# Down projection of a decoder block on one Trainium2 core: another order of its seven products, alternating banks, three sets of split activations

## The chip, the cores and the metric

The kernel runs on one core of one Trainium2 chip. A core has a matrix engine (PE; its weight loads are listed as PEld), a vector engine (DVE), a scalar engine (ACT), a general engine (POOL), and a queue that issues transfers (SP). ACT can issue transfers too; a `q` behind an engine's name in the profile is its queue. All transfers of the core run on the same 16 DMA engines. The metric is the device time of one execution in microseconds. "The clock" is the share of PE's full clock that was granted.

## What is computed

One decoder block over 1024 tokens of width 1024, all in float32: two token mixers, their merge, and a gated feed-forward network. The change lies in the last product of the feed-forward network and in what follows it:

```python
h = rms_norm(x, norm_ffn_g[l]) * (1.0 + sc2) + sh2
gt, up = jnp.split(jnp.einsum("bsd,df->bsf", h, w_ffn_up[l]), 2, axis=-1)
x = x + g2 * jnp.einsum("bsf,fd->bsd", jax.nn.silu(gt) * up, w_ffn_down[l])
...
return rms_norm(x, final_norm_g)
```

The activations `silu(gt) * up` are 1024 × 2816, `w_ffn_down` is 2816 × 1024.

## The kernel before

PE multiplies float32 in three passes: each operand is split into a part that PE takes directly (`hi`) and a rest (`lo`), and hi·hi, lo·hi and hi·lo are summed in PSUM. ACT makes `hi` by a copy, DVE makes `lo` by a subtraction. So every operand costs one ACT and one DVE instruction before PE can use it.

**Seven products.** Up and down projection use a Strassen scheme. Activations and weights are each cut into four quadrants (X11 ... X22 by token half and by even or odd 128-wide block of the inner dimension; W11 ... W22 by the same blocks and by column half), and seven products of sums of quadrants replace eight. For the down projection the operands on the activations' side (X11, X12, X22 and the sums XS1 to XS4) are made by DVE during the up projection, in `act_out`, and stored to seven arrays `act_d` in DRAM. The up projection runs over 22 blocks `f` of 128 inner columns; at odd `f` the sums XS1, XS2, XS4 follow from two successive blocks. ACT's queue issues these stores. The operands on the weights' side are formed from quadrants loaded anew for each product: `WSTEP[i]` names, for product i, a quadrant that is loaded into the buffers `reg0` to `reg5` (`w_fetch`, "fresh"), a second one that is loaded into `other`, and the sign with which they are combined (`w_form`); then ACT and DVE split the result into the tiles `wd`.

**Tiles.** Product i has four tiles t, one for each 128 tokens of a token half, so n = 4i + t runs from 0 to 27. The activations of tile 0 are prepared by `x_first`. For the others `x_fetch` loads 704 KB into `xr` (two buffers), `x_split` makes `xh` on ACT and `xl` on DVE (two sets), and `down_mm` runs 11 × 3 matmuls into one PSUM bank: `xh`·`wd` hi, `xl`·`wd` hi, `xh`·`wd` lo (lines 1345 to 1347). `evict` (and `last` in the last product) adds the bank into the partial sums `U` and `V` (one pair for each t) and, where a quarter of the output is complete, multiplies by the row `g2row`, adds the token rows `x1`, takes the sum of squares on ACT, and multiplies by the row `grow`. When both column halves of a token block are done, `store` takes the inverse root on POOL, scales the two halves on DVE and ACT, and issues two stores from SP.

**Order.** The products run as X11, XS1, XS2, X22, XS3, XS4, X12. The loop below issues, for each n: the fetch for n + 2, token rows, the split of n + 1, the forming of a part of the next product's weights, fetches for the product after, and then the matmuls and the eviction of n. A scheduler then sets the order in which instructions stand on each engine, from the data they depend on, their place in this loop, and simulated durations; each engine works strictly in that order, and SP's queue too.

**Banks.** `bank()` hands out eight banks in turn: pc, pa, pn, pc and then both halves of a pair `mm`, both halves of another pair. A pair is one tile to the scheduler, so whoever writes one half waits until the readers of the other have ended.

**SBUF.** The pool `fp` of the down projection takes the place of the pools of the up projection (`ups`, `trs`), so its first tiles wait until the readers of those are done.

Of the kernel before, what the change touches and what calls it, by code (L numbers as in the profile page):

```python
# [12 lines left out]
OP = mybir.AluOpType  # L13
# [30 lines left out]
X11, XS1, XS2, X22, XS3, XS4, X12 = range(7)  # L44
# [3 lines left out]
WSTEP = ((), (W12, W11, 1), (None, W22, -1), (None, W21, 1), (W22, W12, 1), (W22, None, 0), (W21, None, 0))  # L48
# [7 lines left out]
def hybrid_block(ctx: ExitStack, tc: tile.TileContext, x, c, w_ada, b_ada, norm_mix_g, w_in, b_in,  # L56
# [904 lines left out]
    act_d = [dram.tile([128, 4, FP, 128], F32, name=f"act_d{i}") for i in range(7)]  # L961
# [201 lines left out]
    def act_out(f, half, cg, cu):  # L1163
        ts_ = slice(0, 4) if half is None else slice(2 * half, 2 * half + 2)

        def out(i, t):
            nc.scalar.dma_start(act_d[i][:, ts_, f // 2, :], t.rearrange("p (a c) -> p a c", c=128))
# [9 lines left out]
        out(X22, cg[1])  # L1177
        nc.vector.tensor_add(x21, x21, cg[1])
# [4 lines left out]
        out(XS4, s4)  # L1183

# [21 lines left out]
    def x_first():  # L1206
        out = []
        for a, b in ((0, KT), (KT, FP)):
            raw, hi, lo = (wp.tile([128, KT, 128], dt, name=n, tag=n)[:, 0:b - a, :]
                           for n, dt in (("wraw", F32), ("whi", F32R), ("wlo", F32R)))  # L1210
            nc.sync.dma_start(raw, act_d[X11][:, 0, a:b, :])
# [82 lines left out]
    x1 = [fp.tile([128, D], F32, name=f"x1_{t}") for t in range(8)]  # L1294
    ss = fp.tile([128, 8, 4], F32, name="ssf")
    grow, g2row = (fp.tile([128, D], F32, name=n) for n in ("grow", "g2row"))
# [25 lines left out]
    def x_fetch(n):  # L1322
        raw = fp.tile([128, FP, 128], F32, name="xr", tag="xr", bufs=2)
        nc.sync.dma_start(raw, act_d[n // 4][:, n % 4])
        return raw

    def x_split(raw):
        hi, lo = (fp.tile([128, FP, 128], F32R, name=n, tag=n, bufs=2) for n in ("xh", "xl"))
        nc.scalar.activation(hi, raw, AF.Copy)  # L1329
        nc.vector.tensor_sub(lo, raw, hi.bitcast(F32))  # L1330
        return [(hi[:, k, :], lo[:, k, :]) for k in range(FP)]
# [24 lines left out]
    def store(t):  # L1356
        rsqrt(ss[:, t, 3:4], ss[:, t, 2:3])
        r = ss[:, t, 3:4]
        rows = out2[t * 128:(t + 1) * 128, :]
        for i, (a, b) in enumerate(HALVES):  # L1360
            if i:
                nc.scalar.activation(x1[t][:, a:b], x1[t][:, a:b], AF.Copy, scale=r)
            else:
                nc.vector.tensor_scalar(x1[t][:, a:b], x1[t][:, a:b], r, None, op0=OP.mult)
            nc.sync.dma_start(rows[:, a:b], x1[t][:, a:b])

    LEFT, RIGHT = slice(0, 512), slice(512, 1024)

    def evict(i, t, p):
        if i == 0:  # L1370
            nc.scalar.activation(U[t], p, AF.Copy)
            residual(tok(0, t), LEFT, p)
        elif i == 1:
            nc.scalar.activation(V[t], p, AF.Copy)
        elif i == 2:
            nc.vector.tensor_add(U[t], U[t], p)
            nc.vector.tensor_add(V[t], V[t], U[t])
        elif i == 3:
            nc.vector.tensor_sub(U[t], U[t], p)
        elif i == 4:  # L1380
            x = tok(1, t)
            nc.vector.tensor_add(U[t], U[t], p)
# [5 lines left out]
            nc.vector.scalar_tensor_tensor(ss[:, x, 2:3], ss[:, x, 0:1], EPS, ss[:, x, 1:2], op0=OP.add, op1=OP.add)  # L1388
            nc.vector.tensor_mul(x1[x], x1[x], grow)
            store(x)  # L1390
        elif i == 5:
            x = tok(0, t)
            nc.vector.tensor_add(p, V[t], p)
            residual(x, RIGHT, p)
            square(x, RIGHT, p, 1)
# [83 lines left out]
```

## Time and profile before

| | us |
|---|---|
| median of 3 runs | 1745.27 (1743.14 to 1746.62) |
| the profiled execution | 1743.36 |
| its span, first to last instruction | 1741.6 |
| PE busy | 1678.0 (96%) |
| DVE busy | 1317.1 (76%) |
| ACT busy | 645.0 (37%) |
| mean granted clock of PE | 0.989 |
| first matmul of the down projection | 1475.6 |
| last matmul begins | 1734.65 |

Times in the trace are microseconds from the span's start. A row of the timeline gives the start, the duration, engine, line, operation and tiles (written `out<-in`), and in brackets the idle time of the engine before the instruction and what ended it. Matmuls overlap, so the duration of one (0.4) is longer than the step from one to the next. Engines that are busy are not for that reason what the end waits for: it is what PE waits for in the last 260 us that matters here.

### The profile page before, as it was taken

What the parts mean: (1) busy time and instruction counts of PE and PEld (TensorE: products, weight loads), DVE (VectorE), ACT (ScalarE), POOL (GpSimd) and SP (SyncE); (2) the same over time, 40 slices, a digit from 0 to 9 for tenths busy, and PEclk for the clock granted to TensorE, in tenths of its full rate; (3) what the DMA queues carried; (4) which work ended last, traced back from release to release, by engine and by line L of the source; (5) the groups of instructions that cost most, each with busy time, mean ns of one, the idle gap of its engine ahead of it and who ended that gap; (6) DMA issues with size and microseconds to landing.
All of it is one profiled execution on the core that took longest, in us unless ns stands there. A gap on an engine that the chain in (4) does not pass through costs nothing. (4 is left out here: it accounts for less than half of the span.)

```text
span 1741.6 us, 20859 instructions
## 1 busy us (share of the span) xinstructions
PE 1678.0 (96%) x8237; PEld 1401.4 (80%) x8237; DVE 1317.1 (76%) x1773; ACT 645.0 (37%) x835; POOL 56.9 (3%) x113
## 2 busy tenths in 40 slices
PE   5999999999999999999999998999999999889988
PEld 4788888888988888888888778888888888667767
DVE  7989998987799669445897778777677766586664
ACT  7424435323432253223622475322222222252432
POOL 0000001000001000000000000000000000000000
PEclk9999999999999999999999999999999999899989
DMA  9221120221112212243794642333333333986431
GB/s 318 63 62 49 43 67 25 61 73 49 37 49 62 72 37 61 73 145 97 248 374 158 225 156 89 111 103 107 106 100 103 100 98 101 348 289 244 161 119 65
DMA packets 214825, 211.12 MB, mean 121 GB/s; under 512 B 8503, under 2 KB 173511, under 8 KB 214727
## 3 DMA queue, kind: packets, MB, share of 16 engines
q1 hardware_dynamic: 168199, 168.63, 30.7%
q10 hardware_dynamic: 46528, 41.16, 7.0%
q8 instruction: 64, 1.05, 0.3%
q14 instruction: 34, 0.28, 0.0%
HBM read 168.60 MB, written 41.16 MB: 120 GB/s over the span
## 5 line engine op out<-in xcount | busy, mean ns | idle before, releaser
L395 DVE SCALAR_TENSOR_TENSOR cacc<-a,col,cacc 128x1024 f32<-128x1024 f32 x240 | 306.3, 1283 | 3.9 <-ACT cacc L393 1.4
L165 PE MATMUL mm<-hh,wlo 128*128 128x512 f32 x864 | 271.4, 392 | 1.6 <-DVE wlo L156 1.6
L165 PE MATMUL mm<-hl,whi 128*128 128x512 f32 x864 | 272.7, 393 | 0.0
L165 PE MATMUL mm<-hh,whi 128*128 128x512 f32 x864 | 271.7, 392 | 0.0
L165 PEld LDWEIGHTS mm<-hh,wlo 128*128 128x128 f32 x864 | 160.4, 188 | 33.6 <-DVE wlo L156 2.7
L165 PEld LDWEIGHTS mm<-hl,whi 128*128 128x128 f32 x864 | 161.1, 188 | 32.0 <-issue 0.5
L165 PEld LDWEIGHTS mm<-hh,whi 128*128 128x128 f32 x864 | 160.7, 188 | 31.5
L155 ACT ACTIVATE whi<-wraw 128x1024 fp32r<-128x1024 f32 x61 | 64.7, 1060 | 228.0 <-PE mm L165 180.5
L156 DVE TENSOR_TENSOR wlo<-wraw,whi 128x1024 fp32r<-128x1024 f32 x61 | 74.4, 1219 | 28.7 <-ACT whi L155 25.2
L1123 PE MATMUL mm<-Bh,gh 128*128 128x512 f32 (+1 forms) x192 | 71.6, 376 | 2.9 <-ACT gh L1060 1.5
L1124 PE MATMUL mm<-Bl,gh 128*128 128x512 f32 (+1 forms) x192 | 71.6, 373 | 0.7 <-DVE Bl L1042 0.7
L611 PE MATMUL mm<-wlo,hh 128*128 128x256 f32 x256 | 72.1, 282 | 0.0
L1125 PE MATMUL mm<-Bh,gl 128*128 128x512 f32 (+1 forms) x192 | 71.3, 372 | 0.0
L1329 ACT ACTIVATE xh<-xr 128x1408 fp32r<-128x1408 f32 x27 | 37.0, 1375 | 80.1 <-PE mm L1347 43.9
L542 DVE SCALAR_TENSOR_TENSOR cacc<-qkraw,col,cacc 128x1024 f32<-128x1024 f32 x48 | 61.5, 1281 | 5.0 <-ACT cacc L540 4.5
L1345 PE MATMUL mm<-wd,xh 128*128 128x512 f32 (+1 forms) x143 | 56.9, 399 | 7.5 <-ACT xh L1329 4.4
L1346 PE MATMUL mm<-wd,xl 128*128 128x512 f32 (+1 forms) x143 | 57.0, 398 | 3.6 <-DVE xl L1330 3.6
L1347 PE MATMUL mm<-wd,xh 128*128 128x512 f32 (+1 forms) x143 | 56.5, 395 | 0.0
L610 PE MATMUL mm<-whi,hh 128*128 128x256 f32 x192 | 54.6, 284 | 0.0
L612 PE MATMUL mm<-whi,hl 128*128 128x256 f32 x192 | 54.3, 283 | 0.0
L1330 DVE TENSOR_TENSOR xl<-xr,xh 128x1408 fp32r<-128x1408 f32 x27 | 43.8, 1621 | 9.3 <-ACT xh L1329 9.2
L611 PEld LDWEIGHTS mm<-wlo,hh 128*128 128x128 f32 x256 | 48.7, 190 | 0.0
(487 smaller groups left out, 3885.2 us busy)
## 6 DMA issues: line engine op xcount, KB each, us to landing
wraw<-in_w_in_dram SPq DMA_DIRECT2D x64, 512.0 KB
xr<-act_d SPq DMA_DIRECT2D x27, 704.0 KB
awt<-in_w_ada_dram SPq DMA_DIRECT2D x32, 512.0 KB
act_d<-cg ACTq DMA_DIRECT2D x50, 256.0 KB
graw<-in_w_ffn_up_dram SPq DMA_DIRECT2D x24, 512.0 KB
uraw<-in_w_ffn_up_dram SPq DMA_DIRECT2D x22, 512.0 KB
reg<-in_w_ffn_down_dram SPq DMA_DIRECT2D x20, 512.0 KB
other<-in_w_ffn_down_dram SPq DMA_DIRECT2D x20, 512.0 KB
```

Source lines behind the costliest of these rows:

```text
L155: nc.scalar.activation(hi, raw, AF.Copy)
L156: (eng or nc.vector).tensor_sub(lo, raw, hi.bitcast(F32))
L165: nc.tensor.matmul(flat(acc)[:, a:b], lhs[:, k, :], rhs[k][:, a:b], start=(first and k == 0), stop=(last and k == kt - 1))
L395: nc.vector.scalar_tensor_tensor(acc, a[:, j:j + S], dw_col(j, ct), acc, op0=OP.mult, op1=OP.add)
L542: nc.vector.scalar_tensor_tensor(cv, raw[:, j:j + S], wcol(j), cv, op0=OP.mult, op1=OP.add)
L611: nc.tensor.matmul(o[:, 0:256], hh[k][:, ts_], los[k], start=False, stop=False)
L1123: nc.tensor.matmul(o, a, rh, start=(k == 0), stop=False)
L1124: nc.tensor.matmul(o, a, rl, start=False, stop=False)
L1125: nc.tensor.matmul(o, b, rh, start=False, stop=(k == 3))
L1345: nc.tensor.matmul(o, xh, wh, start=(k == 0), stop=False)
L1346: nc.tensor.matmul(o, xl, wh, start=False, stop=False)
L1347: nc.tensor.matmul(o, xh, wl, start=False, stop=(k == FP - 1))
```

## The change

1. The second product is now X12·W21, which was the last; `WSTEP` follows. Products 0 and 1 then complete the left columns of the first token half, and the last product is XS4·W22, which completes its right columns.
2. `bank()` alternates between single banks and halves of the two pairs.
3. `xh` and `xl` have three buffers; the loop fetches for n + 3 and splits n + 2; `queue_behind` places the first instruction of an eviction behind the split of the next tile on the same engine. `other` has two buffers in place of three.
4. Whole rows of 1024 are scaled by ACT and stored from ACT's queue, one tile later; only the last token block is scaled on both engines and stored in halves from two queues. As before, only the last tile runs as two halves of 256 columns.
5. `act_d` is laid out so that a store writes 2 KB for each partition, and a fetch reads 11 pieces of 512 bytes for each partition (a store wrote four pieces of 512 bytes, a fetch read 5632 bytes in one). In the last block of the up projection XS1, XS2 and XS4 are stored from SP. The first two fetches stand ahead of the other loads, and their buffers lie where the eighth token row buffer lies later.
6. Token rows are fetched by halves where only a half is needed.

```diff
-X11, XS1, XS2, X22, XS3, XS4, X12 = range(7)
+X11, X12, XS1, XS2, X22, XS3, XS4 = range(7)
-WSTEP = ((), (W12, W11, 1), (None, W22, -1), (None, W21, 1), (W22, W12, 1), (W22, None, 0), (W21, None, 0))
+WSTEP = ((), (W21, None, 0), (W12, W11, 1), (None, W22, -1), (None, W21, 1), (W22, W12, 1), (W22, None, 0))
...
-    act_d = [dram.tile([128, 4, FP, 128], F32, name=f"act_d{i}") for i in range(7)]
+    act_d = [dram.tile([128, FP, 512], F32, name=f"act_d{i}") for i in range(7)]
...
-            nc.scalar.dma_start(act_d[i][:, ts_, f // 2, :], t.rearrange("p (a c) -> p a c", c=128))
+            eng = nc.sync if f == FT - 1 and i in (XS1, XS2, XS4) else nc.scalar
+            eng.dma_start(act_d[i][:, f // 2, ts_], t)
...
+        at = tc.cur_priority
+        if f == FT - 1:
+            tc.cur_priority = at + 600
         nc.vector.tensor_add(x21, x21, cg[1])
...
-            other[u] = fp.tile([128, 2, 512], F32, name="other", tag="other", bufs=3)[:, 0:UN[u]]
+            other[u] = fp.tile([128, 2, 512], F32, name="other", tag="other", bufs=2)[:, 0:UN[u]]
...
     def x_split(raw):
-        hi, lo = (fp.tile([128, FP, 128], F32R, name=n, tag=n, bufs=2) for n in ("xh", "xl"))
-        nc.scalar.activation(hi, raw, AF.Copy)
-        nc.vector.tensor_sub(lo, raw, hi.bitcast(F32))
+        hi, lo = (fp.tile([128, FP, 128], F32R, name=n, tag=n, bufs=3) for n in ("xh", "xl"))
+        a = nc.scalar.activation(hi, raw, AF.Copy)
+        v = nc.vector.tensor_sub(lo, raw, hi.bitcast(F32))
+        turned.append((a, v))
...
-            spares.extend([m[1][:, 1], m[1][:, 0], m[0][:, 1], m[0][:, 0], ps_c, ps_n, ps_a, ps_c])
+            spares.extend([m[1][:, 1], ps_n, m[0][:, 1], ps_c, m[1][:, 0], ps_a, m[0][:, 0], ps_c])
...
-    def store(t):
-        rsqrt(ss[:, t, 3:4], ss[:, t, 2:3])
...
+    def store(t, r):
+        nc.scalar.activation(x1[t], x1[t], AF.Copy, scale=r)
+        nc.scalar.dma_start(out2[t * 128:(t + 1) * 128, :], x1[t])
...
         if i == 0:
-            nc.scalar.activation(U[t], p, AF.Copy)
-            residual(tok(0, t), LEFT, p)
+            queue_behind(nc.scalar.activation(U[t], p, AF.Copy), turned[4 * i + t + 1][0])
         elif i == 1:
-            nc.scalar.activation(V[t], p, AF.Copy)
+            queue_behind(nc.vector.tensor_add(p, U[t], p), turned[4 * i + t + 1][1])
+            residual(x, LEFT, p)
+            square(x, LEFT, p, 0)
+            nc.vector.tensor_mul(x1[x][:, LEFT], x1[x][:, LEFT], grow[:, LEFT])
...
+    splits = {0: xp, 1: x_split(raw_x.pop(1))}
     for n in range(N):
         i, t = divmod(n, 4)
-        if n + 2 < N:
-            raw_x[n + 2] = x_fetch(n + 2)
+        if n + 3 < N:
+            raw_x[n + 3] = x_fetch(n + 3)
...
-        later = x_split(raw_x.pop(n + 1)) if n + 1 < N else None
+        if n + 2 < N:
+            splits[n + 2] = x_split(raw_x.pop(n + 2))
```

Three places show how instructions move. The first is SP's queue behind the last weight loads of the up projection. `xr_11654` and `xr_11664` are the raw activations of tiles 1 and 2 before; `xr_11637`, `xr_11639` and `xr_11664` those of tiles 1, 2 and 3 now; `act_d2`, `act_d3` and `act_d6` are the arrays of XS1, XS2 and XS4 now. Before:

```order
L1324 DMA xr_11654<-act_d0_7567 128x1408
L1188 DMA reg0_11640<-in_w_ffn_down_dram 128x2x512
L1188 DMA other_11657<-in_w_ffn_down_dram 128x2x512
L1188 DMA reg1_11641<-in_w_ffn_down_dram 128x2x512
L1188 DMA other_11660<-in_w_ffn_down_dram 128x2x512
L952 DMA g2row_11639<-mrow_d1_7547 128x1024
L1423 DMA x1_0_11629<-x1_d0_7559 128x1024
L1324 DMA xr_11664<-act_d0_7567 128x1408
```

Now:

```order
L1168 DMA act_d2_7569<-cg_11354 128x512
L1168 DMA act_d3_7570<-cg_11354 128x512
L1168 DMA act_d6_7573<-cu_11355 128x512
L1304 DMA xr_11637<-act_d0_7567 128x11x128
L1304 DMA xr_11639<-act_d0_7567 128x11x128
L1193 DMA reg0_11644<-in_w_ffn_down_dram 128x2x512
L1193 DMA reg1_11645<-in_w_ffn_down_dram 128x2x512
L1193 DMA reg2_11646<-in_w_ffn_down_dram 128x2x512
L1193 DMA reg3_11647<-in_w_ffn_down_dram 128x2x512
L952 DMA g2row_11643<-mrow_d1_7547 128x1024
```

The fetch for tile 1, which stood first, has moved behind three stores, and that for tile 2 has moved up from behind five loads to the place right after it; the fetch for tile 3 stands behind `reg4`, `reg5`, `grow` and two blocks of `other` that follow.

The second is ACT at the same place, from the last activation of the up projection on; `xh_11668` before and `xh_11660` now belong to tile 1, `xh_11730` and `xh_11666` to tile 2. Before:

```order
L1158 ACTIVATE cg_11469<-cg_11469 128x512
L1167 DMA act_d3_7570<-cg_11469 512x1x128
L1167 DMA act_d6_7573<-cg_11469 512x1x128
L1167 DMA act_d1_7568<-cg_11354 512x1x128
L1167 DMA act_d2_7569<-cg_11354 512x1x128
L1167 DMA act_d5_7572<-cu_11355 512x1x128
L1371 ACTIVATE U0_11646<-pc_11690 128x512
L1329 ACTIVATE xh_11668<-xr_11654 128x1408
L1202 ACTIVATE wd_11673<-reg0_11640 128x1024
L1202 ACTIVATE wd_11678<-reg1_11641 128x1024
L1329 ACTIVATE xh_11730<-xr_11664 128x1408
```

Now:

```order
L1168 DMA act_d4_7571<-cg_11469 128x512
L1168 DMA act_d1_7568<-cg_11469 128x512
L1339 ACTIVATE xh_11660<-xr_11637 128x1408
L1389 ACTIVATE U0_11650<-pc_11682 128x512
L1339 ACTIVATE xh_11666<-xr_11639 128x1408
L1207 ACTIVATE wd_11670<-reg0_11644 128x1024
L1207 ACTIVATE wd_11674<-reg1_11645 128x1024
```

The split of tile 1 has moved ahead of three stores and of tile 0's eviction, and that of tile 2 ahead of the weights.

The third is DVE in the last two products. `mm_12524` and the first `mm_12525` before hold tiles 21 and 22, and `xl_12870` is the split of tile 23, `xl_12921` that of tile 24; now `mm_12530` holds tile 21 and `xl_12845` is the split of tile 24. Before:

```order
L1393 TENSOR_TENSOR mm_12524<-V1_11651,mm_12524 128x512
L1350 TENSOR_TENSOR mm_12524<-mm_12524,g2row_11639 128x512
L1393 TENSOR_TENSOR mm_12525<-V2_11652,mm_12525 128x512
L1330 TENSOR_TENSOR xl_12870<-xr_12813,xh_12869 128x1408
L1351 TENSOR_TENSOR x1_1_11630<-x1_1_11630,mm_12524 128x512
L1350 TENSOR_TENSOR mm_12525<-mm_12525,g2row_11639 128x512
L1330 TENSOR_TENSOR xl_12921<-xr_12867,xh_12920 128x1408
```

Now:

```order
L1403 TENSOR_TENSOR U1_11651<-U1_11651,mm_12530 128x512
L1404 TENSOR_TENSOR mm_12530<-V1_11655,mm_12530 128x512
L1363 TENSOR_TENSOR U1_11651<-U1_11651,g2row_11643 128x512
L1340 TENSOR_TENSOR xl_12845<-xr_12780,xh_12844 128x1408
L1363 TENSOR_TENSOR mm_12530<-mm_12530,g2row_11643 128x512
L1364 TENSOR_TENSOR x1_3_11632<-x1_3_11632,U1_11651 128x512
```

The splits of tiles 23 and 24 stood behind the start of tile 22's eviction; now that of tile 24 stands inside the eviction of tile 21. On PE the matmuls of these tiles stood in the order 20, most of 22, 21, the rest of 22, a part of 24, 23, the rest of 24; now they stand in the order of n throughout.

More of the change, by code (lines that the diff above doesn't have):

```diff
@@ L1387, in evict @@
             square(x, LEFT, U[t], 0)
[L1388 removed]
+            both(x)
             nc.vector.tensor_mul(x1[x], x1[x], grow)
[L1390 to L1393, printed above, removed]
+            if t == 3:
+                residual(tok(0, t), RIGHT, V[t])
+            return x, rstd(x, 2)
+        elif i == 6:
+            queue_behind(nc.vector.tensor_add(p, V[t], p), turned[4 * i + t + 1][1])
```

108 lines of the change are left out of this document (62 added, 46 removed).

## The prediction

> **What bounds the kernel now.** I read, in this order: the page, the busy time by stretch, the idle gaps of PE in the down projection, and then the queues that end those gaps. A *tile* below is one product on one block of 128 tokens, 33 matmuls; tile n belongs to product n // 4, so there are tiles 0 to 27. The first stretch below is the end of the up projection. The others are tiles 1–3, 4–7, 8–15, 16–19, 20–23 and 24–27, counted as 33 matmuls each, since PE's order before takes most of 22 ahead of 21 and a part of 24 ahead of 23.
>
> ```profile
> span 1741.6 us, 20859 instructions
> 1440.00:1475.00 35.00, 35.00 (x153) 28.38 (x152) 20.52 (x28) 8.96 (x11) 0.00 (x0) 1.00 0.39 126
> 1492.93:1528.67 35.74, 28.50 (x99) 21.64 (x99) 21.70 (x22) 10.93 (x12) 0.00 (x0) 0.85 1.03 396
> 1528.67:1565.27 36.60, 33.50 (x132) 26.12 (x133) 32.78 (x29) 17.91 (x19) 0.00 (x0) 0.92 0.83 273
> 1565.27:1628.85 63.58, 61.84 (x265) 49.60 (x264) 39.34 (x38) 22.87 (x22) 0.00 (x0) 1.00 0.62 212
> 1628.85:1659.52 30.67, 30.67 (x133) 24.91 (x132) 25.00 (x34) 15.24 (x23) 2.91 (x2) 1.00 0.60 204
> 1659.52:1703.29 43.77, 35.64 (x134) 27.71 (x132) 24.93 (x33) 11.87 (x20) 3.51 (x2) 0.88 0.28 90
> 1703.29:1734.93 31.64, 31.25 (x166) 26.37 (x164) 16.73 (x29) 9.61 (x16) 1.62 (x3) 1.00 0.21 74
> ```
>
> After the length come the busy times of PE, PEld, DVE, ACT and POOL, then PE's granted clock, the share of the DMA engines and GB/s. Up to 1475 PE is busy all the time. From tile 1 on it is not, and in three stretches its clock is below 1.00. The measure of an undisturbed tile:
>
> ```profile
> 1565.27 0.40 PE L1345 MATMUL pc<-wd,xh 128*128 128x512 f32 x1
> 1588.28 0.39 PE L1345 MATMUL pc<-wd,xh 128*128 128x512 f32 x1
> ```
>
> These are the first matmuls of tiles 8 and 11: (1588.28 − 1565.27) / 3 = 7.67 us a tile, 0.2325 us a matmul. Against 7.67 a tile the six stretches lose 12.73, 5.92, 2.22, 0.00, 13.09 and 0.96 us, together 34.9. The gaps that start the losses (idle time before the instruction in brackets, and who ended it):
>
> ```profile
> 1492.93 0.49 PE L1345 MATMUL pa<-wd,xh 128*128 128x512 f32 x1 [4.02 <-ACT xh L1329]
> 1494.60 0.80 PE L1346 MATMUL pa<-wd,xl 128*128 128x512 f32 x1 [1.17 <-DVE xl L1330]
> 1514.80 0.50 PE L1345 MATMUL pc<-wd,xh 128*128 128x512 f32 x1 [1.95 <-ACT xh L1329]
> 1528.67 0.80 PE L1345 MATMUL mm<-wd,xh 128*128 128x512 f32 x1 [2.90 <-ACT xh L1329]
> 1541.21 0.50 PE L1345 MATMUL mm<-wd,xh 128*128 128x512 f32 x1 [0.69 <-ACT V L1374]
> 1604.65 0.47 PE L1345 MATMUL mm<-wd,xh 128*128 128x512 f32 x1 [0.87 <-DVE U L1379]
> 1671.28 0.80 PE L1346 MATMUL mm<-wd,xl 128*128 128x512 f32 x1 [1.91 <-DVE xl L1330]
> 1693.39 0.79 PE L1346 MATMUL pc<-wd,xl 128*128 128x512 f32 x1 [3.13 <-DVE xl L1330]
> ```
>
> Two kinds. Most gaps wait for the split of the activations (xh on ACT, xl on DVE), made too late; the clock falls behind each, so that more is lost than the gaps themselves. The gaps of 0.69 and 0.87 wait for the eviction of the tile just before, into the same pair of PSUM banks.
>
> **The change part by part.**
>
> *Three sets of split activations, and the order that comes of them.* The splits themselves stay 27 of each kind:
>
> ```profile
> L1329 ACT ACTIVATE xh<-xr 128x1408 fp32r<-128x1408 f32 x27 | 37.0, 1375 | 80.1 <-PE mm L1347 43.9 <-PE pc L1347 12.5 <-PE pa L1347 7.6
> L1330 DVE TENSOR_TENSOR xl<-xr,xh 128x1408 fp32r<-128x1408 f32 x27 | 43.8, 1621 | 9.3 <-ACT xh L1329 9.2
> ```
>
> ACT does not lack time for them: it sat idle 80.1 us ahead of them, 43.9 of it waiting for PE to finish with one of the two sets. With three sets the split of tile n+3 can start when tile n ends, two tiles (15.3 us) before it is needed, and takes 1.38 + 1.62 = 3.0 us. In DVE's new order the split of tile 24 stands behind the first three instructions of tile 21's eviction, where those of tiles 23 and 24 stood behind the start of tile 22's. PE's order is now strictly 20, 21, 22, 23, 24. So the waits ahead of tiles 3, 4, 22 and 24 (the last is the 3.13 at 1693.39), with the cold stretches behind them, go: tiles 1–3 keep only tile 1's loss, tiles 20–23 lose nothing.
>
> *Alternating banks.* Four gaps (the two shown, one more of each kind) with the slowed matmul behind each: 0.95 to 1.1 us apiece, about 4 us in the sums above. Successive tiles now never share a pair, and each bank has a whole tile for its eviction. The 4 us go. The cover is that tile of 7.67 us against an eviction of a few DVE instructions.
>
> *The order of the products.* X12·W21 comes second. While product 0 runs, only W21 (2.9 MB) is loaded for the next one, where W12 and W11 (5.8 MB) were, and of the token rows come four halves of 256 KB in place of eight rows of 512 KB. In the stretch of tiles 1–3 the DMA share was 1.03: that is where bytes count. DVE's heaviest product, which finishes both column halves of four tiles, moves from product 4 to 5:
>
> ```profile
> L1350 DVE TENSOR_TENSOR pc<-pc,g2row 128x512 f32<-128x512 f32 x5 | 3.5, 695 | 1.4 <-ACT U L1371 1.4
> L1389 DVE TENSOR_TENSOR x<-x,grow 128x1024 f32<-128x1024 f32 x4 | 4.9, 1221 | 0.0
> DVE ssf L1388 <- ACT pa L1354: 0.8, 1, 0.8
> ```
>
> Per tile six operations of the first shape (4.2), one of the second (1.2), a wait for ACT's squares (0.8) and one xl (1.6): 7.8 us against PE's 7.67. DVE runs a little late there, which splits two tiles ahead and free banks cover; without that cover it is the 13 us of tiles 20–23 again.
>
> *Row stores on ACT's queue, whole rows.* 16 issues on SP become 7 of whole rows on ACT, and for the last block a half from each queue. ACT is busy 9.61 of 31.64 us at the end: hidden. The last one, which is not hidden:
>
> ```profile
> 1734.65 0.28 PE L1347 MATMUL mm<-wd,xh 128*128 128x256 f32 x1
> 1737.59 0.72 ACT L1362 ACTIVATE x<-x,ssf 128x512 f32<-128x512 f32 x1 [1.18 <-POOL ssf L111]
> 1738.10 0.81 SPq L1365 DMA_DIRECT2D out_dram<-x  x2
> ```
>
> The end keeps this chain (evict, square, POOL, scale, two stores of 256 KB), with the issues on two queues in place of 0.81 us on one. Between 0.4 gained and 0.4 lost; I take 0.
>
> *2 KB activation stores, three of the last five on SP.* In the up projection PE is busy 35.00 of 35.00 us, so shorter stores cost and bring nothing there. At tile 1 the move is on the path:
>
> ```profile
> 1483.46 0.34 SPq L1324 DMA_DIRECT2D xr<-act_d  x1
> 1486.23 3.50 ACTq L1167 DMA_DIRECT2D act_d<-cg  x4
> 1488.17 0.69 DVE L1182 TENSOR_TENSOR cu<-cg 128x512 f32<-128x512 f32 x1
> 1489.77 1.20 ACTq L1167 DMA_DIRECT2D act_d<-cu  x1
> 1491.51 1.37 ACT L1329 ACTIVATE xh<-xr 128x1408 fp32r<-128x1408 f32 x1
> 1504.88 0.40 PE L1345 MATMUL pn<-wd,xh 128*128 128x512 f32 x1
> 1524.00:1526.00 2.00, 1.78 (x8) 1.12 (x6) 1.03 (x1) 0.18 (x1) 0.00 (x0) 1.00 1.03 411
> 19.00:22.00 3.00, 2.60 (x20) 2.10 (x20) 2.89 (x5) 2.65 (x6) 0.00 (x0) 1.00 1.21 295
> ```
>
> Before, ACT issued five stores (3.50 + 1.20 us) and only then split tile 1, whose raw data SP had fetched from 1483.46 on. Now ACT issues two and is free near 1487.5, but SP has the other three ahead of that fetch, and the third waits for the DVE row that ends at 1488.17 + 0.69 = 1488.86. So the fetch goes out at about 1489.3. It also reads 512-byte pieces now. 1524–1526 moved pieces of 5632 bytes and ran at 411 GB/s; 19–22 was full of 512-byte reads and ran at 295. For 704 KB that is 1.75 and 2.44 us. Issuing, starting and landing add to that: the last store of 256 KB above was issued by 1738.91 and had landed at 1741.6, 2.7 us for a transfer of 0.6, so 2.1 (an estimate from these rows). 1489.3 + 0.3 for the issue + 2.1 + 2.4 is 1494.1; xh ends at 1495.5, xl at 1497.1, where the matmul that waits for it began at 1494.6. Tile 2 started 10.28 us after that matmul (1504.88 − 1494.60, cold clock included), so it now starts at 1507.4: 2.5 us later. Bounds: 0 if the stores don't delay it, 5 if the fetch takes twice its 2.44 and queues besides; I stay near the middle, since each part has a row.
>
> The Trainium skill, "DMA: Bandwidth & Descriptors", section Specifications, gives 512 B as the size from which a transfer runs at line rate. By that rule the fetch would cost no more than before and the sum below would be 0.7 lower. The trace does not agree: 295 against 411 GB/s.
>
> The other fetches: tile 3's stands behind W21, both row vectors and two blocks of W11, 5.0 MB, 12.5 us at 396 GB/s, after tiles 1 and 2's own. From 1493 on (tile 1's data 1 us before they have landed), 2.4 + 12.5 + 2.4 + 1 gives 1511.3, the split 1514.3; PE is ready for tile 3 at 1507.4 + 7.67 = 1515.1. That margin is 0.8 us. Tile 5's is 2.7 by the same count, later ones more, since DMA share falls to 0.6.
>
> *The sum.* Tile 2 starts at 1507.4, 26 tiles of 7.67 are 199.4, and the last, in two halves, adds 0.3: the last matmul ends at 1707.1 instead of 1734.93. That is 27.8 us less, with the same tail. The profiled execution took 1743.36 us, so 1715.6; it lay 1.9 below the median of 1745.27, so I predict 1717.5.
>
> **The rivals.**
>
> 1. *Late fetches* (tiles 3 and 5). For: the 0.8 us margin and a DMA share of 1.03. Against: fewer bytes are asked for early. A miss of 2 us costs these and the cold clock behind them, 2.8 us by tile 1's rows (10.28 − 32 × 0.2325): 4.8, once or twice, 1722 to 1727.
> 2. *DVE stays late*, so the 13.1 us of tiles 20–23 return around products 5 and 6. For: 7.8 us against 7.67. Against: the new order. 1717.5 + 13.1 = 1730.6.
> 3. *The deeper split does nothing*, as there are still only two raw buffers: every split wait stays, the banks bring 4 us and tile 1 takes 2.5 back: 1743.8. Against: a raw buffer is free as soon as its xl is done, far ahead of PE.
> 4. *Bank switching becomes a wait at every tile.* As a mechanism here: the 1.0 us of the bank gaps at 27 switches instead of 4, 1717.5 + 27 = 1744.5, no change. Against: tiles 8 to 11 lie in four different tiles of banks and follow each other at 7.67 us without a gap. The Trainium skill, "TensorE: Matmul & The Clock Gate", section "A second HAM failure mode: psum-queue depth-cycling", tells of a kernel in which cycling through banks made PE idle briefly and its clock swing; by that rule this one would lose its gain, and the trace so far disagrees.
> 5. *Slower:* 512-byte reads make the DMA engines the bound, on all 27 fetches.
>
> ```profile
> DMA packets 23149, 54.00 MB, mean 199 GB/s; under 512 B 1739, under 2 KB 5078, under 8 KB 23136
> ```
>
> That is from 1470 to the end. 27 fetches of 0.72 MB are 19.5 of it; the other 34.5 MB take 86 us at 400 GB/s. Of the 245 us to the last matmul 159 are left, 5.9 us for a fetch. Above 5.9 the gain is gone; at 7 us it would be 27 × 1.1 = 30 us over, 1775. The row gives 2.44.
>
> **How the numbers follow.** The forecast (1712 to 1722) gets 0.52, rival 1 0.20, rival 2 0.13, rival 3 0.03, rival 4 0.03, rival 5 0.04; 0.05 is for still less than 1712 or something between 1731 and 1742. The range 1709 to 1734 holds the forecast and rivals 1 and 2, about 0.86 with the doubts in each size. Within 0.2% means 1741.8 to 1748.8, about what a measurement can tell from no change: rivals 3 and 4. Faster: 0.89, same 0.06, slower 0.05.
>
> **What would show it.** Right: PE's gap ahead of tile 1 is longer than before by 2 to 3 us and ended by xl; no other PE gap above 0.5 us up to the last tile; no gap ended by the eviction of U or V; granted clock 1.00 from the second tile on; the fetch of raw activations leaves SP at about 1489.3; the chain at the end has the same length. Wrong: PE waits for xh ahead of tile 3 or 5 with the DMA share at 1 (rival 1), for xl in product 5 or 6 with DVE busy throughout (rival 2), for xh behind PE's own release (rival 3), gaps at all switches (rival 4), or a DMA share near 1 past tile 8 (rival 5).

## The result, and the profile after

| | before | after |
|---|---|---|
| median of the runs | 1744.84 (1743.14 to 1746.62) | 1716.03 (1715.23 to 1720.23) |
| the profiled execution | 1743.36 | 1720.23 |
| its span | 1741.6 | 1718.5 |
| last matmul begins | 1734.65 | 1711.28 |

The changed kernel is 28.8 us faster: ratio 0.984, 95% interval 0.9821 to 0.9858. The forecast was 1717.5. The profiled execution is the slowest of its four runs, so the traces are compared by stage, and the medians carry the verdict.

From the page of the changed kernel, the length, PE, and the groups of the split and of the matmuls that wait for it:

```profile
span 1718.5 us, 20829 instructions
PE 1671.5 (97%) x8237; PEld 1399.1 (81%) x8237; DVE 1310.7 (76%) x1760; ACT 648.4 (38%) x835; POOL 57.4 (3%) x113
...
L1358 PE MATMUL mm<-wd,xh 128*128 128x512 f32 (+1 forms) x154 | 60.9, 395 | 7.2 <-ACT xh L1339 7.2
...
L1339 ACT ACTIVATE xh<-xr 128x1408 fp32r<-128x1408 f32 x27 | 37.3, 1380 | 70.6 <-DMA xr<-act_d 22.7
L1340 DVE TENSOR_TENSOR xl<-xr,xh 128x1408 fp32r<-128x1408 f32 x27 | 43.8, 1624 | 26.2 <-ACT xh L1339 26.2
```

Before, ACT sat idle 80.1 us ahead of xh, most of it until PE gave a buffer back. Now it is 70.6, and what ended it was this (us, times):

```profile
  DMA xr<-act_d: 22.7, 7
  PE mm L1360: 18.2, 5
  PE pn L1360: 10.4, 3
  PE pc L1360: 6.9, 2
  PE pa L1360: 6.3, 1
```

The fetch from DRAM is the largest single ender, but PE in its four kinds of bank still ends 41.8 us. From tile 4 on no PE gap comes of these waits: the splits are ready in time. The busy times by stretch, cut at the same tiles as before (end of the up projection, tiles 1–3, 4–7, 8–15, 20–23, 24–27; columns as before):

```profile
1440.00:1475.00 35.00, 35.00 (x152) 28.31 (x151) 21.18 (x28) 7.17 (x10) 0.00 (x0) 1.00 0.34 121
1498.33:1526.48 28.15, 26.67 (x100) 20.71 (x100) 17.39 (x14) 13.68 (x14) 0.00 (x0) 0.87 1.07 366
1526.48:1557.28 30.80, 30.80 (x134) 24.78 (x132) 24.77 (x27) 14.44 (x16) 0.00 (x0) 1.00 0.87 264
1557.28:1618.87 61.59, 61.59 (x265) 49.56 (x264) 49.76 (x49) 26.48 (x29) 0.00 (x0) 1.00 0.90 292
...
1649.67:1680.47 30.80, 30.80 (x133) 24.78 (x132) 23.71 (x32) 12.37 (x20) 4.13 (x3) 1.00 0.41 127
1680.47:1711.56 31.09, 31.09 (x166) 26.36 (x164) 19.05 (x31) 12.21 (x19) 4.45 (x5) 1.00 0.22 86
```

From tile 4 on PE is busy all the time at clock 1.00, 7.70 us a tile. Tiles 20–23 take 30.80 where they took 43.77, tiles 1–3 28.15 where they took 35.74. Only three of PE's gaps are left, all ahead of tiles 1 and 3:

```profile
1498.33 0.79 PE L1358 MATMUL mm<-wd,xh 128*128 128x512 f32 x1 [7.23 <-ACT xh L1339]
1499.99 0.79 PE L1359 MATMUL mm<-wd,xl 128*128 128x512 f32 x1 [0.87 <-DVE xl L1340]
1518.92 0.50 PE L1359 MATMUL mm<-wd,xl 128*128 128x512 f32 x1 [0.61 <-DVE xl L1340]
```

The first gap has grown from 4.02 to 7.23 us. SP's queue and ACT show why:

```profile
1489.63 1.06 SPq L1168 DMA_DIRECT2D act_d<-cg  x2
1491.08 0.32 SPq L1168 DMA_DIRECT2D act_d<-cu  x1
1491.45 0.58 SPq L1304 DMA_DIRECT2D xr<-act_d  x1
1496.90 1.38 ACT L1339 ACTIVATE xh<-xr 128x1408 fp32r<-128x1408 f32 x1 [12.21 <-DMA xr<-act_d]
```

The fetch of tile 1 leaves right behind the third store, as foretold, and ACT waits for its data.

### The profile page after: what moved, and what is told of

It reads as the page before. It is cut to its first block, busy times and chain, and to the rows that moved or that the text cites. A ratio compares the mean times of both kernels' runs of the same rounds, so it can differ in the third digit from the quotient of the medians.

```text
span 1718.5 us, 20829 instructions
## 1 busy us (share of the span) xinstructions
PE 1671.5 (97%) x8237; PEld 1399.1 (81%) x8237; DVE 1310.7 (76%) x1760; ACT 648.4 (38%) x835; POOL 57.4 (3%) x113
## 5 line engine op out<-in xcount | busy, mean ns | idle before, releaser
L1358 PE MATMUL mm<-wd,xh 128*128 128x512 f32 (+1 forms) x154 | 60.9, 395 | 7.2 <-ACT xh L1339 7.2
L1339 ACT ACTIVATE xh<-xr 128x1408 fp32r<-128x1408 f32 x27 | 37.3, 1380 | 70.6 <-DMA xr<-act_d 22.7
L1359 PE MATMUL mm<-wd,xl 128*128 128x512 f32 (+1 forms) x154 | 61.0, 396 | 1.5 <-DVE xl L1340 1.5
L1360 PE MATMUL mm<-wd,xh 128*128 128x512 f32 (+1 forms) x154 | 60.5, 393 | 0.0
```

The lines of the kernel that those rows point to most:

```text
L1358: nc.tensor.matmul(o, xh, wh, start=(k == 0), stop=False)
L1359: nc.tensor.matmul(o, xl, wh, start=False, stop=False)
L1360: nc.tensor.matmul(o, xh, wl, start=False, stop=(k == FP - 1))
```

## The experiments

Each kernel was timed with the kernel before on the same chip; the ratio is to that. The first letter says what was edited: `u` the changed kernel with a part undone, `b` the kernel before with a part done alone, `early` the changed kernel with more.

| run | edit | median us | before, same call | ratio (95%) |
|---|---|---|---|---|
| after_again | none | 1718.03 | 1743.81 | 0.9846 (0.9833–0.9860) |
| u_act | XS stores on ACT | 1714.08 | 1743.81 | 0.9827 (0.9812–0.9841) |
| u_layout | former layout of `act_d` | 1717.24 | 1743.81 | 0.9846 (0.9832–0.9859) |
| early | and tile 1 fetched early | 1710.72 | 1743.81 | 0.9803 (0.9790–0.9816) |
| early_pool | and XS stores on POOL | 1707.12 | 1744.00 | 0.9788 (0.9773–0.9802) |
| u_sets | two sets | 1717.62 | 1744.00 | 0.9848 (0.9833–0.9863) |
| u_banks | former banks | 1721.10 | 1744.00 | 0.9869 (0.9853–0.9886) |
| u_order | former order of products | 1722.78 | 1744.00 | 0.9876 (0.9861–0.9891) |
| u_sets_banks | two sets and former banks | 1761.99 | 1744.75 | 1.0095 (1.0080–1.0111) |
| b_sets | three sets alone | 1726.16 | 1744.75 | 0.9887 (0.9871–0.9904) |
| b_banks | new banks alone | 1725.98 | 1744.75 | 0.9889 (0.9874–0.9904) |
| b_banks_sets | both | 1721.12 | 1744.75 | 0.9863 (0.9848–0.9878) |

Runs with the same number in the column of before were timed together. Where no run of the changed kernel stands beside a run, it is put at 0.9846 of before: 1717.2 beside 1744.00, 1717.9 beside 1744.75. The medians of its two measurements would put it anywhere from 1715.2 to 1718.2 beside 1744.00, so a difference of 1 to 2 us from it is none that these medians can tell.

### What holds tile 1

**The changed kernel again.**

> The changed kernel once more, so that the others of this call stand beside it on the same chip. Theory R: the 2.2 us by which its profiled execution lay behind at the start of the down projection (first matmul there at 1477.79 against 1475.60 before, lost between 1040 and 1070, where no instruction was changed) belong to that one execution; then the start lies within 0.5 us of 1475.6 here and the time is 1715 to 1716. Theory C: they come with the changed kernel; then the start is again near 1477.8 and the time is 1716 to 1720.

Neither: the first matmul of the down projection began at 1476.61, between the two. Over the fourteen profiled executions of all kernels PE's first matmul of the up projection's products (line 1123) begins between 1039.22 and 1042.89, with nothing changed up to there. So that 2 us is spread from one execution to the next, and theory C is not borne out: over all kernels the first matmul of the down projection begins between 1474.37 and 1478.21. Below, times are counted from the first matmul of the down projection where it matters. The tile took 7.67 us here, so the 7.70 above belongs to its execution too.

**The three stores back on ACT's queue.**

```diff
-            eng = nc.sync if f == FT - 1 and i in (XS1, XS2, XS4) else nc.scalar
+            eng = nc.scalar
```

> The changed kernel, but the last stores of XS1, XS2 and XS4 stand on ACT's queue again, so that nothing stands ahead of tile 1's fetch on SP. Theory S (the three stores delay the fetch): in the profile of the changed kernel the fetch left SP at 1491.45, right after the third store (1491.08 + 0.32), and xh started at 1496.90, 5.45 later. Before, the fetch left 0.9 us after the last matmul of the up projection began, here 1485.7; the data are there at 1491.1. ACT then waits for its own third store behind the DVE row that ends at 1491.05, so xh runs from 1491.4 to 1492.8 and xl ends at 1494.4. The matmul that waits for xl begins at 1494.4 instead of 1499.99: 5.5 us less than the changed kernel in the same call, near 1710.5. Theory B (the reads of 512 bytes are what takes the time, wherever the fetch stands): the fetch takes longer than 5.45 beside the other loads, and less than 2 us are gained. Theory N: something else ends tile 1's wait, no change.

Its SP, ACT and PE:

```profile
1472.12 0.57 SPq L1304 DMA_DIRECT2D xr<-act_d  x1
...
1489.65 0.82 ACTq L1168 DMA_DIRECT2D act_d<-cu  x1
1490.57 1.38 ACT L1339 ACTIVATE xh<-xr 128x1408 fp32r<-128x1408 f32 x1 [7.31 <-PE pc L1360]
...
1493.66 0.80 PE L1359 MATMUL mm<-wd,xl 128*128 128x512 f32 x1 [0.94 <-DVE xl L1340]
...
1512.19 0.50 PE L1358 MATMUL mm<-wd,xh 128*128 128x512 f32 x1 [0.77 <-ACT xh L1339]
1513.86 0.51 PE L1359 MATMUL mm<-wd,xl 128*128 128x512 f32 x1 [1.16 <-DVE xl L1340]
```

Theory S holds, and the surprise is the first row: without the stores the fetch leaves at 1472.12, not at 1484. Its buffer lies in a place that is free at least 11.7 us before the last matmul of the up projection begins (1483.80), and only the stores ahead of it on SP kept it back: by 17.9 us, counted from the first matmul (13.66 after it in the changed kernel, 4.24 ahead of it here). Now ACT is the limit, as expected: xh starts 0.1 after the last store's issue. The matmul that waits for xl comes 17.30 us after the first of the down projection, against 22.20: 4.9 us gained, 5.5 expected. The medians gained 4.0 (1718.03 to 1714.08): with an earlier tile 1, tile 3's data are late by more, and its two gaps with the slow matmuls behind them cost 2.5 us instead of 0.9.

**The former layout.**

```diff
-    act_d = [dram.tile([128, FP, 512], F32, name=f"act_d{i}") for i in range(7)]
+    act_d = [dram.tile([128, 4, FP, 128], F32, name=f"act_d{i}") for i in range(7)]
```

(and the store and the two fetches to match)

> The changed kernel with the former layout of the activations in DRAM: a store writes four pieces of 512 bytes for each partition, a fetch reads 5632 bytes in one. Theory S: the fetch of tile 1 gets 0.7 us shorter (1.75 against 2.44 by the rates 411 and 295 GB/s) and the gap of 0.6 us ahead of tile 3 goes, but the three stores ahead of it on SP take 0.5 to 1.2 us each to issue (before: 0.52 to 1.27 on ACT) in place of 0.33, so that it leaves up to 2 us later: within 1.5 us of the changed kernel, either way. Theory B (reads of 512 bytes hold back more than this one fetch; SP took 4.6 us to issue three loads of token rows behind such fetches): 2 us or more are gained, and those issues fall below 1 us. Theory U (shorter stores hold back the up projection): the down projection starts later by 1 us or more.

The medians lie 0.8 apart with overlapping ranges: no difference that the runs can tell, as theory S has it. The fetch left at 1490.86 and xh started 5.35 us later, where it took 5.45 and, in the run again, 5.77 with pieces of 512 bytes: of the 0.7 us that I had priced 0.1 to 0.4 came. The stores right ahead of it write four pieces of 512 bytes each now and took 0.57 to 0.82 us to issue in place of 0.32 to 0.34; counted from the first matmul of the down projection, the fetch left 0.5 us later. Theory U falls: PE is busy without a gap from 1100 to 1470 with either layout. The transfers themselves: the changed kernel, then this one, each while the first two fetches pass (1493–1496) and while the next pass among other loads (1510–1513):

```profile
1493.00:1496.00 3.00, 0.00 (x0) 0.00 (x0) 0.00 (x0) 0.00 (x0) 0.00 (x0) 0.94 0.96 269
...
1510.00:1513.00 3.00, 3.00 (x14) 2.42 (x13) 0.50 (x1) 0.60 (x1) 0.00 (x0) 1.00 1.09 326
```

```profile
1493.00:1496.00 3.00, 0.00 (x0) 0.00 (x0) 0.00 (x0) 0.00 (x0) 0.00 (x0) 0.55 1.02 353
...
1510.00:1513.00 3.00, 3.00 (x15) 2.43 (x14) 0.00 (x0) 0.00 (x0) 0.00 (x0) 1.00 1.03 407
```

At a full DMA share, 326 GB/s against 407: the price of short reads is real (0.80), and tile 3's gap did go. The Trainium skill, "DMA: Bandwidth & Descriptors", section "Why small descriptors are slow (HBM only)", gives a fixed overhead of about three cycles for each packet; for 512 bytes that is 16 of 19 cycles, an estimate of 0.84 for such pieces alone, near the 0.80 of this row, which holds other loads besides; the same page's 512 bytes for full rate does not agree with it. Theory B's second sign came too: the issue of a token row behind such a fetch, the changed kernel first, then this one:

```profile
1504.91 4.63 SPq L1380 DMA_DIRECT2D x<-x_d  x1
```

```profile
1503.58 0.34 SPq L1380 DMA_DIRECT2D x<-x_d  x1
```

But SP's lost time is not what PE waits for, so nothing came of it.

**Tile 1 fetched early.** The XS stores are on ACT, and tile 1's raw data go to two buffers `wraw` outside the pool that is rebuilt:

```diff
-    raw_x = {n: x_fetch(n) for n in (1, 2)}
+    raw_x = {1: x_early(1), 2: x_fetch(2)}   # x_early: [0:8] and [8:11] into two tiles of wp, tag "wraw"
```

> As the run with the three stores on ACT, and tile 1's raw activations are fetched into the two buffers that held tile 0's, which are read for the last time at 1479.87 in the profile of the changed kernel; the fetch can leave SP near 1480, and with both ordinary raw buffers free the fetch of tile 3 moves up behind two weight loads. Theory S2 (with the three stores gone from SP, tile 1 waits for ACT, which stands behind the last store and thereby behind DVE's last row at 1491.05): xh still starts at 1491.4, xl's first part ends at 1493.6; tile 1 gains 6.4 us on the changed kernel, 0.9 more than the run with the stores on ACT, and tile 3's gap of 0.6 us goes with the 0.3 of cold clock behind it: near 1708.7. Theory F (the fetch itself is the limit in that run): this one is 3 us or more faster than it. Theory D (loads moved up collide): the weights of the second product come later, PE waits for wd at tile 4, and nothing more is gained than 5.5.

```profile
1488.16 0.40 ACTq L1168 DMA_DIRECT2D act_d<-cu  x1
1488.66 1.47 ACT L1348 ACTIVATE xh<-wraw 128x1024 fp32r<-128x1024 f32 x2 [6.89 <-PE pc L1369]
```

Theory S2: xh still starts just behind ACT's last store, the matmul that waits for xl comes 16.16 us after the first (17.30 with the stores on ACT), and tile 3's gap is gone. Against that run 3.4 us are gained, more than the 1.8 expected, because tile 3 had lost 2.5 there, not 0.9. So F's threshold of 3 us is met without F's cause: the fetch was not the limit.

**The XS stores on POOL's queue.**

```diff
+            eng = nc.gpsimd if f == FT - 1 and i in (XS1, XS2, XS4) else nc.scalar
```

> As the run with the early fetch, but the last stores of XS1, XS2 and XS4 are issued from POOL's queue, so that neither SP nor ACT waits behind them. In the profile of that run ACT's second-last free moment before the split of tile 1 was 1486.44 and the split began at 1488.66, behind the stores; DVE's last row ended at 1488.12 and its part of the split began at 1489.75. Theory S (the stores on ACT are what is left at tile 1): xh ends at 1487.6, xl's first part starts at 1488.15 and ends at 1489.4; tile 1 starts without a gap where tile 0 ends (1488.2) and its second matmul at 1489.4 in place of 1491.03: 1.6 us less and about 1 us less of cold clock, 2 to 3 us faster than the early fetch alone. Theory K (POOL's issues are slow or meet DVE at a shared port): DVE's rows get longer there or the stores land late, and nothing is gained.

```profile
1489.78 1.33 POOL L1168 DMA_DIRECT2D act_d<-cg  x2 [436.58 <-DVE cg L1182]
...
1492.11 0.50 PE L1368 MATMUL mm<-wd,xl 128*128 128x512 f32 x1 [0.89 <-DVE xl L1349]
```

Tile 1 now starts without a gap, and 0.89 ahead of its second matmul is all that PE idles in the down projection. From its first to its last matmul 221.41 us pass, 224.41 with the early fetch alone, 232.57 in the changed kernel run again. DVE's rows beside POOL's issues keep their 0.69 us. At 1707.12 this is the fastest kernel of the study: theory S. Its interval overlaps that of the early fetch, so the last 3 us rest on the traces of one execution each.

### What takes the other waits away

**Two sets in place of three.**

```diff
-        hi, lo = (fp.tile([128, FP, 128], F32R, name=n, tag=n, bufs=3) for n in ("xh", "xl"))
+        hi, lo = (fp.tile([128, FP, 128], F32R, name=n, tag=n, bufs=2) for n in ("xh", "xl"))
...
-            splits[n + 2] = x_split(raw_x.pop(n + 2))
+            splits[n + 1] = x_split(raw_x.pop(n + 1))
```

(and the fetches two tiles ahead in place of three)

> The changed kernel with two sets of xh and xl in place of three, the split issued one tile ahead and the fetch two, as before; order of products, banks and all else stay as changed. Theory D (the deeper split carries most of the gain, as the prediction has it): the waits for xh and xl that began the losses at tiles 3 and 4 and in tiles 20 to 23 come back, 4.9 to 6.2 us at each of 3 and 4 and 13.1 at the others by the rows of before, of which the new order of PE and the lighter start keep a part away: 10 to 22 us slower than the changed kernel, 1727 to 1739. Theory O (order of products and banks carry it, and two sets would do): within 3 us of the changed kernel, near 1717.

1717.62, where the changed kernel would take 1717.2, and 232.24 us from the first to the last matmul of the down projection, 232.57 in the changed kernel run again: theory D, the prediction's, falls. No wait comes back, and that at tile 3 is 1.17 in place of 0.61 to 0.82. In this kernel two sets do.

**The former banks.**

```diff
-            spares.extend([m[1][:, 1], ps_n, m[0][:, 1], ps_c, m[1][:, 0], ps_a, m[0][:, 0], ps_c])
+            spares.extend([m[1][:, 1], m[1][:, 0], m[0][:, 1], m[0][:, 0], ps_c, ps_n, ps_a, ps_c])
```

> The changed kernel with the former order of banks: pc, pa, pn, pc, both halves of a pair, both halves of the other. Theory P (as the prediction has it): four gaps of 0.7 to 0.9 us that wait for an eviction, with a slowed matmul behind each, 0.95 to 1.1 apiece: 4 us slower than the changed kernel. Theory Q (the scheduler answers a shared pair by turning tiles round on PE, as it did before with tiles 21 and 22, and the split of a later tile is then waited for): more than 7 us slower. Theory E (evictions stand earlier on DVE now that splits are made two tiles ahead): less than 2 us.

3.9 us slower (235.92 from first to last matmul, 3.4 more), P's size, but not P's cause: no gap waits for an eviction. The waits are for xl: a longer one at tile 3, and two new ones at tiles 6 and 16, which PE takes ahead of 5 and 15 in this program. That is theory Q's cause at P's size. The longest:

```profile
1535.31 0.51 PE L1359 MATMUL mm<-wd,xl 128*128 128x512 f32 x1 [2.00 <-DVE xl L1340]
```

**The former order of products.**

```diff
-X11, X12, XS1, XS2, X22, XS3, XS4 = range(7)
+X11, XS1, XS2, X22, XS3, XS4, X12 = range(7)
```

(with `WSTEP`, the evictions and whole token rows to match)

> The changed kernel with the former order of the seven products (X12 last), its evictions and its whole token rows; three sets, alternating banks, layout and stores stay as changed. Theory B (bytes at the start count): tile 3's fetch now stands behind 6.0 MB in place of 5.0 (five and a half blocks of W12, two of W11, two row vectors, two token rows), 2.6 us more at 396 GB/s, on a fetch that already comes 0.6 us late; and the weights of the second product need 5.8 MB in place of 2.9, through two buffers of `other`, by tile 4. A gap of 3 us ahead of tile 3 and one of 2 to 6 ahead of tile 4, with cold clock behind each: 5 to 12 us slower than the changed kernel. Theory N (the order only moves work about): within 2 us.

5.6 us slower (236.98 from first to last matmul, 4.4 more), at the low end of theory B. The edit takes back the token rows by halves too, so the 5.6 belong to both. Tile 3 waits, tile 4 does not; PE takes parts of tiles 4, 5 and 6 in turn there:

```profile
1520.37 0.50 PE L1358 MATMUL mm<-wd,xh 128*128 128x512 f32 x1 [2.29 <-ACT xh L1339]
1522.03 0.50 PE L1359 MATMUL mm<-wd,xl 128*128 128x512 f32 x1 [1.16 <-DVE xl L1340]
```

Some 27 us had come (1744.00 to 1717.2), and single parts taken back cost 0.4, 3.9 and 5.6. Either the rest lay elsewhere, or parts cover for each other. Hence the next four.

**Each alone, on the kernel before; and both taken back.** The banks are the line above, the other way round; for the sets `bufs` is 3, `other` has two buffers, and

```diff
-        later = x_split(raw_x.pop(n + 1)) if n + 1 < N else None
+        if n + 2 < N:
+            splits[n + 2] = x_split(raw_x.pop(n + 2))
```

(and the fetches three tiles ahead in place of two)

> The kernel before with three sets of xh and xl, splits two tiles ahead and fetches three (`other` has two buffers for it); order of products, banks, layout and stores as before. Theory D (the prediction's: the deeper split carries most): the waits ahead of tiles 3 and 4 and in 20 to 23 go, 15 to 25 us faster than before. Theory R (either of two covers is enough in tiles 20 to 24: a third set, or banks that let PE take the tiles in order): 9 to 14 us faster, all of it in tiles 20 to 24; tiles 1 to 7 lose what they lost, since fetches set them. Theory T (PE's order, turned by shared pairs, is what is waited for): PE's order is still turned at tiles 5, 6, 14, 15 and 20 to 23, and less than 6 us are gained.

> The kernel before with the new order of banks alone. PE takes the tiles in order of n in this kernel but for a part of tile 5 or 7. Theory D: the four gaps that wait for an eviction go, 3 to 5 us faster, and the waits for xl in tiles 20 to 23 stay. Theories R and T: the losses of tiles 20 to 24 (13.1 us) go too, as the split of a tile is no longer waited for ahead of its turn: 13 to 18 us faster than before, and tiles 1 to 4 lose what they lost.

> The kernel before with both, the new order of banks and the three sets. Theory D: 22 to 28 us faster than before, the whole gain of the change. Theory R: no more than 3 us faster than the better of the two alone, and what is missing to the changed kernel (9 to 13 us) is lost at tiles 1 to 5, which only the order of products relieves. Theory T: the same as the new banks alone.

> The changed kernel with two sets of xh and xl (splits one tile ahead) and the former order of banks together; taken back alone, the sets cost nothing and the banks 3.4 us. Theory R (each covers for the other): with both gone the waits for xl in tiles 20 to 24 are back, with those of the bank gaps: 12 to 20 us slower than the changed kernel, 1729 to 1737. Theory A (the two simply add): 3 to 5 us slower, near 1721.

The sets alone bring 18.6 us, the banks alone 18.8, both together 23.6, and without both the changed kernel is 44 us slower than with them, slower even than before. The parts do not add: each alone brings most of what both bring. That is theory R, but its sizes were missed (18.6 where 9 to 14 were expected, 44 where 12 to 20 were, 4.8 beyond the better one where 3 were, and 3.2 missing to the changed kernel where 9 to 13 were), and two of theory D's hold by size (18.6 in 15 to 25, 23.6 in 22 to 28). What decides is where the time went. With the banks alone, and two sets, tiles 5 to 26 lose nothing (tiles counted as 33 matmuls each), where theory D had the waits of 20 to 23 stay; tiles 1 to 4 lose 16.1 us, 17.6 before. With the sets alone tiles 1 to 4 lose 13.5, and 4.7 are lost at tiles 15, 21 and 22.

The mechanism is to be read in ACT's splits. Before, those of tiles 22 to 26:

```profile
1667.44 1.38 ACT L1329 ACTIVATE xh<-xr 128x1408 fp32r<-128x1408 f32 x1 [5.02 <-issue]
1687.06 2.64 ACT L1329 ACTIVATE xh<-xr 128x1408 fp32r<-128x1408 f32 x2 [10.54 <-PE mm L1347]
1708.65 1.38 ACT L1329 ACTIVATE xh<-xr 128x1408 fp32r<-128x1408 f32 x1 [13.95 <-PE mm L1347]
1711.48 1.38 ACT L1329 ACTIVATE xh<-xr 128x1408 fp32r<-128x1408 f32 x1 [1.45 <-PE pc L1347]
```

With the new banks alone, those of tiles 23 to 26:

```profile
1670.08 1.38 ACT L1329 ACTIVATE xh<-xr 128x1408 fp32r<-128x1408 f32 x1 [1.47 <-PE mm L1347]
1677.74 1.38 ACT L1329 ACTIVATE xh<-xr 128x1408 fp32r<-128x1408 f32 x1 [0.68 <-PE pn L1347]
1685.46 1.38 ACT L1329 ACTIVATE xh<-xr 128x1408 fp32r<-128x1408 f32 x1 [3.33 <-issue]
1693.14 1.38 ACT L1329 ACTIVATE xh<-xr 128x1408 fp32r<-128x1408 f32 x1 [3.28 <-issue]
```

Two tiles in a row share a pair in the former order. In the kernel before the scheduler kept such tiles in order up to tile 20, and there lie the gaps that wait for an eviction; behind tile 20 it put a tile of the other pair ahead: PE takes most of 22, then 21, then the rest of 22. Both sets are then held until both tiles end, and come free at nearly the same time: two splits one right behind the other (x2), after 10.54 us in which ACT sat idle, and PE waits for them. With alternating banks PE takes tiles 20 to 24 in order, and a set comes free every 7.7 us. With a third set PE's order is still turned, at tiles 4 to 6 and 13 to 16 too, but one split lies ready. Tiles 20 to 25 lose 13.8 us before, nothing with the banks, 3.8 with the sets; the eviction gaps go with either, all but 0.17 us. With neither, in the changed kernel, the waits are these:

```profile
1560.43 0.80 PE L1359 MATMUL pc<-wd,xl 128*128 128x512 f32 x1 [6.61 <-DVE xl L1340]
```

```profile
1706.64 0.80 PE L1359 MATMUL pc<-wd,xl 128*128 128x512 f32 x1 [4.21 <-DVE xl L1340]
```

The first is the wait of tile 8, taken ahead of 7, the second that of 24, taken ahead of 23. That kernel loses more than the kernel before, which has two sets and shared pairs too: 22.5 us at tiles 4 to 9 against 5.9, and 21.1 at 20 to 25 against 13.8. PE's order is turned in more places there (tiles 5 to 10 and 21 to 26); why the scheduler turns it there and not in the kernel before stays open. No run leaves out `queue_behind`: without it in the evictions the program differs in one place alone, where ACT makes the split of tile 1 behind the eviction of tile 0 and not ahead of it.

## Why the prediction was right, and where it was wrong

- **The sum** was right: 1717.5 against 1716.03, and 1718.03 in the run again; 27.8 us forecast, 28.8 and 25.8 measured. In the profile the last matmul ended at 1711.56, by the clock of before (2.19 us earlier, the distance of the first matmuls) at 1709.4 and not at 1707.1. The 2.3 us are 0.6 at tile 2, 0.9 at tile 3 and 0.8 of the slower tile in that execution. That the first median came out below the forecast all the same is luck: the profiled execution lay 4.2 above its median, where the forecast had that of before 1.9 below its own. A sum over losses that vanish does not depend on what makes them vanish; that is why a wrong assignment left no mark on it.
- **Three sets** is the step that failed. I gave them four waits with their cold stretches, and wrote that PE's strict order comes of them. The strict order comes of the banks, and without the third set the changed kernel measures the same (1717.62). Alone on the kernel before they do bring 18.6 us, with PE's order still turned, but the waits ahead of tiles 3 and 4 do not go by them: tiles 1 to 4 still lose 13.5 of 17.6 us.
- **Alternating banks** were sized too small: 4 us for four gaps. They bring 18.8 alone, 13.8 of it at tiles 20 to 25, where they straighten PE's order. Taken back from the changed kernel the cost is 3.9 us, by waits for splits of tiles taken ahead of their turn and not by the eviction gaps that I had priced.
- **The order of products** had no price of its own, only fewer bytes ahead of tile 3. With the token rows by halves it is worth 5.6 us, there.
- **Tile 1**: the fetch left at 1491.45, by the clock of before at 1489.26, forecast 1489.3; tile 2 started at 1508.0, forecast 1507.4. The 2.5 us was right against before (3.1, and 2.8 in the run again); PE's two gaps ahead of tile 1 came to 8.10 us, 2.9 more than before. The stores cost more than that, 4.0, since the new buffers would have let the fetch leave 18 us sooner, which I did not see: I took the 1483.46 of before for the earliest.
- **Tile 3's margin** of 0.8 us was missed by 0.6, with 0.3 of slow matmuls behind it: rival 1 in small. In the run again it was 0.82. The split of tile 3 began at 1513.6 by the clock of before, and 1511.3 was the time counted for its data.
- **512-byte reads**: the rate was right (295 forecast from, 269 to 326 read); of the 0.7 us at tile 1 the run with the former layout shows 0.1 to 0.4. The 411 GB/s that it was priced against came from a stretch of 216 packets and 0.82 MB, 3.8 KB each on average, and not of 5632 bytes alone. Rival 5 is out, since PE has no gap past tile 3 and the DMA share falls to 0.41 by tiles 20–23; but its sign came in part: the share is 0.90 in tiles 8–15, where it was 0.62.
- **Rival 2** is out: DVE's 7.8 us in product 5 cost nothing, with three sets or two. **Rival 3** has its first half: in the changed kernel the deeper split does nothing that the runs can tell. Its reason fails, as the sets bring 18.6 us on the kernel before with the same two raw buffers. **Rival 4** is out too: the clock stays at 1.00 through every switch of banks from tile 4 on. (The Trainium skill, "TensorE: Matmul & The Clock Gate", section "A second HAM failure mode: psum-queue depth-cycling", is thus not borne out here.)
- **Row stores and tail**: the chain at the end keeps its length within 0.3 us:

```profile
1711.28 0.28 PE L1360 MATMUL pc<-wd,xh 128*128 128x256 f32 x1
...
1714.22 0.72 ACT L1438 ACTIVATE x<-x,ssf 128x512 f32<-128x512 f32 x1 [1.18 <-POOL ssf L111]
...
1714.73 0.35 SPq L1437 DMA_DIRECT2D out_dram<-x  x1
1714.97 0.34 ACTq L1439 DMA_DIRECT2D out_dram<-x  x1
```

From the last matmul to the end of the span 7.2 us, 6.95 before. The two issues now overlap, and that brought nothing.

## What to carry to other kernels

When several parts of a change guard against the same wait, undoing one shows little: here 0.4 and 3.9 us taken one by one, 44 together. Doing each alone on the kernel before shows it (18.6, 18.8, and 23.6 for both). Ask of every wait for a buffer not only how many there are but in what order they are given back; an order turned by a shared tile elsewhere can make two come free at once. And ahead of a transfer on a queue in order, look when its buffer is free, not when it left before: the stores put ahead of it cost the difference.

## What the runs showed of the hardware that was not expected

- Issuing one load on SP took 4.63 us behind a fetch of 1408 pieces of 512 bytes, 0.34 behind the same bytes in 128 pieces: it is SP's queue that stands still, and whatever comes next on it.
- Issuing a store from POOL took 0.54 to 0.78 us (1.33 for the two in the row above), where ACT and SP took 0.32 to 0.34 for the same store in the changed kernel.
- PE's wait for the split of the first weights of the up projection ended anywhere within 3.7 us (1039.22 to 1042.89) in fourteen executions and lasted 0.95 to 3.32 us, though nothing ahead of it had changed: a spread as large as several of the effects here.
